# One ring of PSUM banks, weight splits in pieces, decay differences on ScalarE, and wide products in every second pair of the gate stage

## The chip, the cores and the metric

The kernel runs on one core of one Trainium2 chip. The metric is device time in microseconds (us), the median of several executions. Engines are named as in the profile: PE (TensorE, matmuls), PEld (its weight loads), DVE (VectorE), ACT (ScalarE), POOL (GpSimd), SP (SyncE, which issues all transfers here).

## The reference, cut to what matters

One layer of a hybrid decoder block on 256 positions of width 1024, in float32:

```python
h    = rms_norm(x, norm1_g)
proj = h @ w_in                          # q | k | v | z | xBC | dt | gate_attn | gate_ssd
A    = causal attention(rms_norm(q), rms_norm(k), v)        # 16 heads, ALiBi, one block of 256 keys
# state-space mixer, 8 groups of 4 heads, one chunk of 256 positions:
xs, bm, cm = split(silu(causal_conv(xBC)))
a    = softplus(dt + dt_bias) * -exp(a_log);  acum = cumsum(a)
lmat = exp(where(causal, acum[t] - acum[s], -inf))          # the decay between two positions
y    = einsum(cm @ bm.T, lmat, xs * dt) + d_skip * xs;  y = y * silu(z)
S    = y * rsqrt(mean(y * y, group) + eps) * ssd_norm_g
x    = x + (sigmoid(g_attn) * (A @ w_attn_o) + sigmoid(g_ssd) * (S @ w_ssd_o)) @ w_out
# expert layer: 8 heads pick 16 of 16384 single-neuron experts
xn   = rms_norm(x, norm2_g);  q = xn @ w_peer_q
eidx, gw = top16 over sums of top16(q1 @ keys1), top16(q2 @ keys2), softmax
x    = x + sum over picks of gw * gelu(xn . u_tab[eidx]) * v_tab[eidx]
```

## The kernel before

**Matmuls and weight splits.** Every large product is done in float32r with both operands split into a high and a low part, in three terms (high x high, high x low, low x high). The weights stream in as 392 tiles of 128 x 1024 (512 KB each), in the order of use. `ahead` (L115) keeps the loads five and the splits three tiles ahead of PE: ACT copies a tile to its high part `wh` (L128), and DVE (L135) or, for one tile in four and later in three, POOL (L130) subtracts it to get the low part `wl`. The activations' two parts lie beside each other (`hT`, `xx`: 8 blocks of 2 x 256 columns).

**Two forms of a product.** In the narrow form (`product_T` L162, `u_pair` L1040) each of a tile's eight weight blocks makes three matmuls of 256 columns, 24 in all. In the wide form (`wide`, L176) each high block makes one matmul of 512 columns over both parts of the activations, and each low block one of 256, 16 in all. The wide form leaves its result in two halves of a bank, which ACT (a copy) and DVE (an add) then bring together.

**Stages.** From 14 to 295 us: for each of eight groups the projections q/k, v, x, B/C and z, each followed by generators (`attention`, `conv`, `zgate`, `ssd`) that `tick` advances one step per half tile of products, so that the small operations of attention and mixer lie between the large products on PE. After the eight groups come the gate projections, the output projections, the norm and the query projection. From 438 us: the products with `u_tab`, 64 pairs of tiles. While the top-16 picks are made, pairs 0 to 26 take the wide form (`u_wide`, L1029); after that comes the gate stage (pairs 27 to 63, 638 to 883 us), in which each pair is narrow (`u_pair`) and is followed by up to one `gate_group` (L1077): matmuls of one-hot matrices (`oh`, `og`, made by DVE, L1067 and L1072) into a bank `psg`, by which DVE multiplies the gelu already stored (L1088) or which ACT stores (L1090). The last 348 us are the products with `v_tab` (L1136 to L1138).

**PSUM.** `ps_tile` (L229) hands out the eight banks from three rings: 3 "mm" for the large products, 2 "tr" for transposes, 3 "at" for the other small matmuls. A tile waits until the readers of the one that had its bank before are done. In the "tr" ring, the first transposed attention weights `pp` of a group, the second `pp`, and the transposed mixer output `pty` follow one another.

**The mixer's decay.** In `ssd` (L644), `ar` is the cumulative sum along the row, broadcast by a DMA from memory, and `nac` the negated sum of each position. `seg` (L668) makes min(ar + nac, 0) on DVE, `damp` (L674) the exponential on ACT and the product with the masked scores on DVE. Later DVE scales `y` by the group norm `ry` (L734), which POOL computes as a power (L223).

**Order of the work.** Engines work off their queues in order. The framework's scheduler sets the order on DVE, ACT and POOL; PE follows the program text.

Of the kernel before, what the change touches and what calls it, by code (L numbers as in the profile page):

```python
# [9 lines left out]
F32 = mybir.dt.float32  # L10
# [50 lines left out]
def tile_hybrid_block(ctx: ExitStack, tc: tile.TileContext, x, n1g, wblk, wdt, qkg, cw, cb, dtb,  # L61
# [167 lines left out]
    def ps_tile(tag, name):  # L229
        return psum.tile([128, 512], F32, name=name, tag=tag, bufs={"mm": 3, "tr": 2, "at": 3}[tag])  # L230

    with tc.tile_pool(name="pa", bufs=1) as pa, ExitStack() as ctx2:
# [76 lines left out]
        def turned_x(xn, tt):  # L309
            pt = ps_tile(("tr", "at")[tt], "ptx").rearrange("p (c t) -> p c t", c=4)  # L310
# [105 lines left out]
        nac = pa.tile([128, 2, 32], F32, name="nac")  # L416
# [11 lines left out]
        def decay():  # L428
# [34 lines left out]
            ps = ps_tile("tr", "psdtn")  # L463
# [31 lines left out]
            pc = ps_tile("at", "pscum")  # L495
# [3 lines left out]
            pr = ps_tile("at", "pscumT")  # L499
# [4 lines left out]
            A.activation(nac, pc[:, :64].rearrange("p (a h) -> p a h", a=2), AF.Copy, scale=-1.0)  # L504
# [5 lines left out]
        def attention(g):  # L510
# [19 lines left out]
            pt = half(ps_tile("tr", "ptq"))  # L530
# [42 lines left out]
            def turn(hh):  # L573
                pp[hh] = ps_tile("tr", "pp")
# [30 lines left out]
            po = ps_tile("at", "po")  # L605
# [38 lines left out]
        def ssd(g):  # L644
# [10 lines left out]
            pt = half(ps_tile("tr", "ptx"))  # L655
# [31 lines left out]
            pc = ps_tile("at", "pcb")  # L687
# [14 lines left out]
            py = half(ps_tile("at", "py"))  # L702
# [12 lines left out]
            pt = half(ps_tile("tr", "ptn"))  # L715
# [21 lines left out]
            pt = half(ps_tile("tr", "pty"))  # L737
# [93 lines left out]
        def norm2(tt, po):  # L831
# [3 lines left out]
            yield from norm_T(pm, tt, ss2[:, tt:tt + 1], n2, xh, xl, ("tr", "at")[tt])  # L835
# [54 lines left out]
    def head_scores(h, ps):  # L890
        qT = tk.tile([128, 2, T], F32, name="pqT", tag="pqT")
        if h == 0:
# [3 lines left out]
            ps = ps_tile("tr", "pqt").rearrange("p (c t) -> p c t", c=2)  # L896
# [13 lines left out]
        p2 = ps_tile("tr", "pss").rearrange("p (a n) -> p a n", a=4)  # L910
# [90 lines left out]
    def turned_picks(tt, srcs):  # L1001
# [4 lines left out]
        pt = ps_tile("tr", "ptk").rearrange("p (a t) -> p a t", a=4)  # L1006
# [96 lines left out]
    for jp in range(64):  # L1103
        (u_wide if start is None else u_pair)(jp)
# [17 lines left out]
    py = [ps_tile(("at", "at", "at", "mm")[i], f"py{i}") for i in range(4)]  # L1122
# [94 lines left out]
```

## Time and profile before

| | |
|---|---|
| Median of 3 executions | 1237.66 us (1237.06 to 1240.53) |
| Profiled execution | 1237.04 us, of which the span from first to last instruction is 1235.3 us |
| PE busy | 1217.6 us (99%) |
| DVE busy | 930.1 us (75%) |
| ACT busy | 668.9 us (54%) |
| POOL busy | 233.6 us (19%) |
| PE's share of the chain that ended last | 84% (DVE 9%, ACT 3%) |

A matmul's end is modelled and matmuls overlap, so the busy time of PE says little by itself. What a matmul costs is read from the time between the starts of neighbours, and what PE loses from its idle time before an instruction.

### The profile page before, as it was taken

What the parts mean: (1) busy time and instruction counts of PE and PEld (TensorE: products, weight loads), DVE (VectorE), ACT (ScalarE), POOL (GpSimd) and SP (SyncE); (2) the same over time, 40 slices, a digit from 0 to 9 for tenths busy, and PEclk for the clock granted to TensorE, in tenths of its full rate; (3) what the DMA queues carried; (4) which work ended last, traced back from release to release, by engine and by line L of the source; (5) the groups of instructions that cost most, each with busy time, mean ns of one, the idle gap of its engine ahead of it and who ended that gap; (6) DMA issues with size and microseconds to landing.
All of it is one profiled execution on the core that took longest, in us unless ns stands there. A gap on an engine that the chain in (4) does not pass through costs nothing.

```text
span 1235.3 us, 21224 instructions
## 1 busy us (share of the span) xinstructions
PE 1217.6 (99%) x8152; PEld 1093.6 (89%) x8152; DVE 930.1 (75%) x1721; ACT 668.9 (54%) x1108; POOL 233.6 (19%) x112
## 2 busy tenths in 40 slices
PE   9999999999999999999999999999999999999998
PEld 7989989898888988888889999999988888888887
DVE  6888989799566677899898898999755555555554
ACT  5666666677644455656655454444445445445442
POOL 3212223221232222233232222222000000000000
PEclk9999999999999999999999999999999999999999
DMA  5444444444555464546544444444555555555553
GB/s 197 162 170 148 154 170 155 155 147 137 177 205 188 136 222 159 197 161 202 195 163 171 171 159 166 155 155 154 180 195 187 201 191 188 200 192 189 200 189 120
DMA packets 60342, 215.07 MB, mean 174 GB/s; under 512 B 7600, under 2 KB 8144, under 8 KB 60112
## 3 DMA queue, kind: packets, MB, share of 16 engines
q1 hardware_dynamic: 60240, 213.71, 50.4%
q8 instruction: 64, 1.05, 0.3%
q14 instruction: 38, 0.31, 0.1%
HBM read 212.60 MB, written 1.08 MB: 173 GB/s over the span
## 4 chain that ended last, share of the span: by engine, by line
PE 84%; DVE 9%; ACT 3%; issue 2%; DMA 1%; POOL 0%; DVEq 0%; POOLq 0%
PE py L1136 9%; PE py L1138 9%; PE py L1137 9%; PE psu L189 7%; PE psu L1047 6%; PE psu L1048 6%; PE psu L1049 6%; PE psu L191 3%; PE psqk L207 2%; PE psg L1085 2%; PE pS L189 2%; PE psg L189 2%; PE psq L189 2%; DVE acc L626 2%; DVE wl L135 2%
## 5 line engine op out<-in xcount | busy, mean ns | idle before, releaser
L128 ACT ACTIVATE wh<-wr 128x1024 fp32r<-128x1024 f32 x390 | 411.0, 1055 | 221.1 <-PE py L1138 83.2
L135 DVE TENSOR_TENSOR wl<-wr,wh 128x1024 fp32r<-128x1024 f32 x312 | 383.0, 1229 | 134.8 <-ACT wh L128 133.8
L130 POOL TENSOR_TENSOR wl<-wr,wh 128x1024 fp32r<-128x1024 f32 x78 | 201.5, 2583 | 525.7 <-ACT wh L128 446.3
L1136 PE MATMUL py<-wh,hh 128*128 128x512 f32 x512 | 199.2, 389 | 0.0
L1137 PE MATMUL py<-wl,hh 128*128 128x512 f32 x512 | 199.2, 389 | 0.0
L1138 PE MATMUL py<-wh,hl 128*128 128x512 f32 x512 | 199.2, 389 | 0.0
L1047 PE MATMUL psu<-xx,wh 128*128 128x256 f32 x592 | 170.0, 287 | 0.0
L1048 PE MATMUL psu<-xx,wh 128*128 128x256 f32 x592 | 167.4, 283 | 0.0
L1049 PE MATMUL psu<-xx,wl 128*128 128x256 f32 x592 | 167.3, 283 | 0.0
L1138 PEld LDWEIGHTS py<-wh,hl 128*128 128x128 f32 x512 | 96.1, 188 | 20.1
L1136 PEld LDWEIGHTS py<-wh,hh 128*128 128x128 f32 x512 | 96.1, 188 | 19.8
L1137 PEld LDWEIGHTS py<-wl,hh 128*128 128x128 f32 x512 | 96.1, 188 | 19.8
L1048 PEld LDWEIGHTS psu<-xx,wh 128*128 128x128 f32 x592 | 113.5, 192 | 0.0
L1049 PEld LDWEIGHTS psu<-xx,wl 128*128 128x128 f32 x592 | 113.4, 192 | 0.0
L1047 PEld LDWEIGHTS psu<-xx,wh 128*128 128x128 f32 x592 | 113.3, 191 | 0.0
L189 PE MATMUL psu<-xx,wh 128*128 128x512 f32 x432 | 109.3, 393 | 0.5 <-DVE gA L1037 0.5
L189 PEld LDWEIGHTS psu<-xx,wh 128*128 128x128 f32 x432 | 77.3, 189 | 14.6 <-DVE gA L1037 1.1
L1128 ACT ACTIVATE hh<-gA 128x512 fp32r<-128x512 f32 x64 | 40.4, 632 | 88.8 <-PE py L1137 88.7
L1129 DVE SCALAR_TENSOR_TENSOR hl<-gA,hh 128x512 fp32r<-128x512 f32 x64 | 44.4, 694 | 52.3 <-ACT hh L1128 52.3
L191 PEld LDWEIGHTS psu<-xx,wl 128*128 128x128 f32 x432 | 59.0, 190 | 4.3
L191 PE MATMUL psu<-xx,wl 128*128 128x256 f32 x432 | 60.4, 282 | 0.0
L1072 DVE TENSOR_TENSOR og<-oh,g 128x1024 f16<-128x1024 f16 x64 | 58.0, 946 | 1.0
(324 smaller groups left out, 2211.7 us busy)
## 6 DMA issues: line engine op xcount, KB each, us to landing
wr<-in_u_tab SPq DMA_DIRECT2D x128, 512.0 KB, 3.3
wr<-in_v_tab SPq DMA_DIRECT2D x128, 512.0 KB, 3.2
wr<-in_wblk SPq DMA_DIRECT2D x88, 512.0 KB, 3.3
wr<-in_wso SPq DMA_DIRECT2D x16, 512.0 KB, 4.0
wr<-in_wpq SPq DMA_DIRECT2D x16, 512.0 KB, 3.8
ar<-acT SPq DMA_DIRECT2D x8, 512.0 KB, 4.9
wr<-in_wao SPq DMA_DIRECT2D x8, 512.0 KB, 3.4
wr<-in_wou SPq DMA_DIRECT2D x8, 512.0 KB, 3.5
```

Of the source, the lines that this page charges most:

```text
L128: K(A.activation(h, r, AF.Copy))
L130: state["pool"] = nc.gpsimd.tensor_tensor(lo, r, f32(h), op=OP.subtract)
L135: state["wl"] = K(V.tensor_tensor(lo, r, f32(h), op=OP.subtract))
L189: mm(ps, h[:, c], x[:, k], start=k == 0, stop=k == 8 * n - 1)
L191: mm(ps[:, 1], lo[:, c], x[:, k, 0], start=False, stop=False)
L1047: mm(ps[:, jj], h[:, c], xh[:, c], start=c == 0, stop=False)
L1048: mm(ps[:, jj], h[:, c], xl[:, c], start=False, stop=False)
L1049: mm(ps[:, jj], lo[:, c], xh[:, c], start=False, stop=c == 7)
L1072: V.tensor_tensor(og[:, i], oh[:, 1], g2[:, i, t].rearrange("p (g e) -> p g e", e=2)[:, :, None, :] .to_broadcast([128, 4, 128, 2]), op=OP ...
L1136: mm(o, hh[:, jj, s], h[:, c], start=j == 0, stop=False)
L1137: mm(o, hh[:, jj, s], lo[:, c], start=False, stop=False)
L1138: mm(o, hl[:, jj, s], h[:, c], start=False, stop=j == 127)
```

## The change

The two rings "tr" (2 banks) and "at" (3) become one ring "ax" of 5; all tiles of both take the tag "ax", as do the four `py` accumulators of the last stage (one of them was "mm"). POOL's splits are made in four pieces of 256 columns, each an instruction, and PE waits for the piece that it reads. The decay difference moves from DVE to ACT: relu(acum[s] - ar), and the exponential takes the scale -1. The scaling of `y` moves from DVE to ACT. In the gate stage every second pair (27, 29, ... 63) takes the wide form; where gate values are already stored, its gelu goes to a scratch tile and is multiplied in.

```diff
             if i == 121 or (2 < i < n_u + 128 and not 116 <= i < 124 and i % (3 if i >= 88 else 4) == PS[i >= 88]):
-                state["pool"] = nc.gpsimd.tensor_tensor(lo, r, f32(h), op=OP.subtract)
-                if behind:
-                    after(state["pool"], behind[1])
+                for c in range(4):
+                    q = slice(256 * c, 256 * c + 256)
+                    state["pool"] = nc.gpsimd.tensor_tensor(lo[:, q], r[:, q], f32(h)[:, q], op=OP.subtract)
+                    if behind and c == 0:
+                        after(state["pool"], behind[1])
...
-        return psum.tile([128, 512], F32, name=name, tag=tag, bufs={"mm": 3, "tr": 2, "at": 3}[tag])
+        return psum.tile([128, 512], F32, name=name, tag=tag, bufs={"mm": 3, "ax": 5}[tag])
...
-            A.activation(nac, pc[:, :64].rearrange("p (a h) -> p a h", a=2), AF.Copy, scale=-1.0)
+            A.activation(pac, pc[:, :64].rearrange("p (a h) -> p a h", a=2), AF.Copy)
...
             def turn(hh):
-                pp[hh] = ps_tile("tr", "pp")
+                pp[hh] = ps_tile("ax", "pp")
...
-                V.tensor_scalar(e[:, 0:256], ar[:, r], nac[:, 0, h:h + 1], 0.0, op0=OP.add, op1=OP.min)
-                V.tensor_scalar(e[:, 256:384], ar[:, r, 128:256], nac[:, 1, h:h + 1], 0.0, op0=OP.add, op1=OP.min)
+                A.activation(e[:, 0:256], ar[:, r], AF.Relu, bias=pac[:, 0, h:h + 1], scale=-1.0)
+                A.activation(e[:, 256:384], ar[:, r, 128:256], AF.Relu, bias=pac[:, 1, h:h + 1], scale=-1.0)
...
-                A.activation(e, e, AF.Exp)
+                A.activation(e, e, AF.Exp, scale=-1.0)
...
-                V.tensor_scalar(y[:, tt], y[:, tt], rr[:, tt:tt + 1], None, op0=OP.mult)
+                A.activation(y[:, tt], y[:, tt], AF.Copy, scale=rr[:, tt:tt + 1])
...
         (_, _, dst), = halves(2 * jp, 2 * jp + 2)
+        td = done["t"]
+        to = pb.tile([128, 2, T], F32, name="gel", tag="gel", bufs=2) if td else dst
         for jj in range(2):
             ps = half(ps_tile("mm", "psu"))
             wide(ps, 1, xx)
-            A.activation(dst[:, jj], ps[:, 1], AF.Copy)
-            V.tensor_tensor(dst[:, jj], dst[:, jj], ps[:, 0], op=OP.add)
-        A.activation(dst, dst, AF.Gelu)
+            A.activation(to[:, jj], ps[:, 1], AF.Copy)
+            V.tensor_tensor(to[:, jj], to[:, jj], ps[:, 0], op=OP.add)
+        if td < T:
+            A.activation(dst[:, :, td:], to[:, :, td:], AF.Gelu)
+        if td:
+            A.activation(to[:, :, :td], to[:, :, :td], AF.Gelu)
+            V.tensor_tensor(dst[:, :, :td], dst[:, :, :td], to[:, :, :td], op=OP.mult)
...
-        (u_wide if start is None else u_pair)(jp)
+        (u_wide if start is None or jp % 2 else u_pair)(jp)
...
-    py = [ps_tile(("at", "at", "at", "mm")[i], f"py{i}") for i in range(4)]
+    py = [ps_tile("ax", f"py{i}") for i in range(4)]
```

**Order on ACT, group 0's mixer.** The place is where the broadcast sums `ar` of group 0 have landed and its decay is made; `e` is the decay, `acc` and `u` the convolution, `qkT` the turned q and k of group 1, `wh` a weight's high part. Before:

```order
L620 ACTIVATE u<-psxs_796 128x512
L622 ACTIVATE acc<-psxs_796,cbs,cws 128x256 x2
L676 ACTIVATE e<-e 128x384 x2
L128 ACTIVATE wh_987<-wr_881 128x1024
L538 ACTIVATE qkT<-ptq,qkgs 128x256 x2
L630 ACTIVATE th<-acc 128x512
L128 ACTIVATE wh_993<-wr_935 128x1024
```

The same place on ACT now:

```order
L623 ACTIVATE u<-psxs_805 128x512
L625 ACTIVATE acc<-psxs_805,cbs,cws 128x256
L675 ACTIVATE e<-ar,pac 128x256
L676 ACTIVATE e<-ar,pac 128x128
L675 ACTIVATE e<-ar,pac 128x256
L676 ACTIVATE e<-ar,pac 128x128
L625 ACTIVATE acc<-psxs_805,cbs,cws 128x256
L541 ACTIVATE qkT<-ptq,qkgs 128x256 x2
L128 ACTIVATE wh_999<-wr_890 128x1024
L633 ACTIVATE th<-acc 128x512
L680 ACTIVATE e<-e 128x384 x2
```

Four differences (L675, L676) are new on ACT, and the two exponentials (L680, before L676) now stand behind half a convolution, `qkT`, a weight and `th`.

**Order on DVE, at group 0's mixer output.** `yT` is what PE's transposes `ptn` wait for, `bc` the convolved B and C of group 1. Before:

```order
L135 TENSOR_TENSOR wl_1126<-wr_985,wh_1125 128x1024
L626 SCALAR_TENSOR_TENSOR acc<-u,cws,acc 128x253
L671 TENSOR_SCALAR e<-ar,nac 128x256
L712 SCALAR_TENSOR_TENSOR yT<-xs,dks,py 128x256 x2
L633 SCALAR_TENSOR_TENSOR bc<-th,acc 128x512
```

The same place on DVE now:

```order
L138 TENSOR_TENSOR wl_1138<-wr_997,wh_1137 128x1024
L572 RECIPROCAL rs<-sums 128x2
L636 SCALAR_TENSOR_TENSOR bc<-th,acc 128x512
L716 SCALAR_TENSOR_TENSOR yT<-xs,dks,py 128x256 x2
L728 TENSOR_TENSOR y<-ptn,zz 128x512
```

The difference `e` in front of `yT` is gone, and `bc` has come in front of it.

**Order on DVE, gate stage.** The place is between the multiplications by 144 and by 152 columns of gate values; `gel` is the scratch tile, `oh` and `og` the one-hot matrices. Now:

```order
L1098 TENSOR_TENSOR gA_7841<-gA_7841,psg 128x34x4
L1077 TENSOR_TENSOR oh<-iot,selT 128x2048
L1043 TENSOR_TENSOR gel<-gel,psu 128x256
L1082 TENSOR_TENSOR og<-oh,g_5558 128x1024 x2
L138 TENSOR_TENSOR wl_9831<-wr_9743,wh_9830 128x1024
L1043 TENSOR_TENSOR gel<-gel,psu 128x256
L1098 TENSOR_TENSOR gA_5555<-gA_5555,psg 128x64x4 x2
```

Before, the same rows stood there without the two additions L1043. On PE nothing changes its place: the sequence of tiles that its matmuls write is the same, with 16 matmuls in place of 24 for each tile of 19 pairs. On SP one `ar` transfer goes one place earlier.

## Rows read from the trace of the kernel before

**Rows 1.** Stretches: busy time of each engine (instructions), granted clock, DMA share, GB/s.

```profile
...
14.00:295.00 281.00, 271.65 (x2214) 254.28 (x2213) 239.82 (x489) 189.69 (x389) 69.78 (x38) 0.99 0.45 155
...
638.00:883.00 245.00, 245.00 (x2293) 243.49 (x2292) 219.80 (x305) 117.34 (x221) 63.58 (x25) 1.00 0.48 163
```

**Rows 2.** What PE waited for: us in total, times, longest us.

```profile
...
PE ptn L718 <- DVE yT L712: 3.0, 1, 3.0
PE pp L576 <- DVE yy L749: 3.0, 3, 1.9
...
PE pp L576 <- ACT pT L580: 1.2, 1, 1.2
...
PE pp L576 <- ACT wh L128: 0.9, 1, 0.9
PE pp L576 <- ACT acc L622: 0.7, 1, 0.7
```

**Rows 3.** Timeline 153 to 158 us: start, us, engine, line, operation, tiles [idle <-releaser].

```profile
...
156.09 0.87 DVE L749 SCALAR_TENSOR_TENSOR yy<-pty,sg,yy 128x256 fp32r<-128x256 f32 x2
...
157.10 0.52 PE L576 MATMUL pp<-ident,p 128*128 128x128 f32 x3 [1.93 <-DVE yy L749]
```

**Rows 4.** Timeline 80 to 85.5 us.

```profile
...
81.19 2.44 POOL L130 TENSOR_TENSOR wl<-wr,wh 128x1024 fp32r<-128x1024 f32 x1 [15.39 <-ACT wh L128]
81.35 2.43 DVE L671 TENSOR_SCALAR e<-ar,nac 128x256 f32<-128x256 f32 x1
...
83.70 0.86 DVE L712 SCALAR_TENSOR_TENSOR yT<-xs,dks,py 128x256 f32<-128x256 f32 x2
```

**Rows 5.** Timeline 641 to 643.2 us, PE: a narrow product.

```profile
...
641.16 0.28 PE L1047 MATMUL psu<-xx,wh 128*128 128x256 f32 x1
...
642.96 0.28 PE L1047 MATMUL psu<-xx,wh 128*128 128x256 f32 x1
```

**Rows 6.** Timeline 500 to 512 us, PE: wide products.

```profile
...
502.20 2.00 PE L189 MATMUL psu<-xx,wh 128*128 128x512 f32 x8
...
507.79 2.00 PE L189 MATMUL psu<-xx,wh 128*128 128x512 f32 x8
```

**Rows 7.** Groups by form: busy us, mean ns of one | idle before, releasers.

```profile
...
L128 ACT ACTIVATE wh<-wr 128x1024 fp32r<-128x1024 f32 x390 | 411.0, 1055 | 221.1 <-PE py L1138 83.2 <-PE psu L1048 37.0 <-issue 32.0
...
L130 POOL TENSOR_TENSOR wl<-wr,wh 128x1024 fp32r<-128x1024 f32 x78 | 201.5, 2583 | 525.7 <-ACT wh L128 446.3 <-ACT gA L1055 13.4 <-DVE og L1072 8.2
...
L1047 PE MATMUL psu<-xx,wh 128*128 128x256 f32 x592 | 170.0, 287 | 0.0
...
L189 PE MATMUL psu<-xx,wh 128*128 128x512 f32 x432 | 109.3, 393 | 0.5 <-DVE gA L1037 0.5
...
L191 PE MATMUL psu<-xx,wl 128*128 128x256 f32 x432 | 60.4, 282 | 0.0
...
L1037 DVE TENSOR_TENSOR gA<-gA,psu 128x256 f32<-128x256 f32 x54 | 22.1, 409 | 6.1 <-ACT gA L1036 6.1
...
L1036 ACT ACTIVATE gA<-psu 128x256 f32<-128x256 f32 x54 | 20.5, 379 | 31.2 <-PE psu L189 31.2
...
L671 DVE TENSOR_SCALAR e<-ar,nac 128x256 f32<-128x256 f32 x32 | 17.6, 550 | 3.5 <-DMA ar<-acT 3.5
...
L571 ACT ACTIVATE p<-p,rs 128x256 f32<-128x256 f32 x16 | 7.9, 495 | 0.0
...
L571 ACT ACTIVATE p<-p,rs 128x128 f32<-128x128 f32 x16 | 6.3, 391 | 0.8 <-DVE rs L569 0.8
...
L362 POOL TENSOR_TENSOR wl<-wr,wh 128x512 fp32r<-128x512 f32 x2 | 2.5, 1290 | 2.5 <-ACT wh L336 2.5
```

**Rows 8.** What ACT waited for, 14 to 295 us.

```profile
...
ACT e L676 <- DVE e L672: 13.1, 9, 2.8
```

**Rows 9.** Timeline 781 to 785 us: the gate stage.

```profile
...
780.91 3.50 DVE L1072 TENSOR_TENSOR og<-oh,g 128x1024 f16<-128x1024 f16 x2
...
781.32 2.54 POOL L130 TENSOR_TENSOR wl<-wr,wh 128x1024 fp32r<-128x1024 f32 x1 [8.19 <-ACT wh L128]
```

More of the change, by code (lines that the diff above doesn't have):

```diff
@@ L309, in turned_x @@
         def turned_x(xn, tt):
-            pt = ps_tile(("tr", "at")[tt], "ptx").rearrange("p (c t) -> p c t", c=4)
+            pt = ps_tile("ax", "ptx").rearrange("p (c t) -> p c t", c=4)
             for c in range(4):
@@ L415, in tile_hybrid_block @@
         dth = pa.tile([128, 2, 32], F32, name="dth")
-        nac = pa.tile([128, 2, 32], F32, name="nac")
+        pac = pa.tile([128, 2, 32], F32, name="pac")
         dram = ctx.enter_context(tc.tile_pool(name="dr", bufs=1, space=bass.MemoryType.DRAM))
@@ L462, in decay @@
             yield
-            ps = ps_tile("tr", "psdtn")
+            ps = ps_tile("ax", "psdtn")
             for tt in range(2):
@@ L494, in decay @@
                 yield
-            pc = ps_tile("at", "pscum")
+            pc = ps_tile("ax", "pscum")
             mm(pc[:, 0:32], mask[:, 0:128], av[:, 0], start=True, stop=True)
@@ L498, in decay @@
             mm(pc[:, 32:64], mask[:, 0:128], av[:, 1], start=False, stop=True)
-            pr = ps_tile("at", "pscumT")
+            pr = ps_tile("ax", "pscumT")
             mm(pr[:32, 0:128], av[:, 0], mask[:, 0:128], start=True, stop=True)
@@ L529, in attention @@
             yield
-            pt = half(ps_tile("tr", "ptq"))
+            pt = half(ps_tile("ax", "ptq"))
             for tt in range(2):
@@ L548, in score @@
                         if a == 0:
-                            sc[hh] = ps_tile("at", "sc")
+                            sc[hh] = ps_tile("ax", "sc")
                         mm(sc[hh][:, a:b], q[:, a:a + 128], k[:, :b - a], start=True, stop=True)
@@ L604, in attention @@
             v = vsb[g // 2]
-            po = ps_tile("at", "po")
+            po = ps_tile("ax", "po")
             for i, (qs, ks_) in enumerate((((0, 256), (0, 256)), ((128, 256), (256, 384)))):
@@ L654, in ssd @@
             yield
-            pt = half(ps_tile("tr", "ptx"))
+            pt = half(ps_tile("ax", "ptx"))
             for tt in range(2):
@@ L686, in ssd @@
             yield
-            pc = ps_tile("at", "pcb")
+            pc = ps_tile("ax", "pcb")
             mm(pc[:, 0:256], bc[:, 0, 0:128], bc[:, 1], start=True, stop=True)
@@ L701, in ssd @@
             yield
-            py = half(ps_tile("at", "py"))
+            py = half(ps_tile("ax", "py"))
             for ct in range(2):
@@ L714, in ssd @@
             yield
-            pt = half(ps_tile("tr", "ptn"))
+            pt = half(ps_tile("ax", "ptn"))
             for tt in range(2):
@@ L733, in ssd @@
             for tt in range(2):
-                V.tensor_scalar(y[:, tt], y[:, tt], rr[:, tt:tt + 1], None, op0=OP.mult)
+                A.activation(y[:, tt], y[:, tt], AF.Copy, scale=rr[:, tt:tt + 1])
             yield
             yield
-            pt = half(ps_tile("tr", "pty"))
+            pt = half(ps_tile("ax", "pty"))
             for c in range(2):
@@ L834, in norm2 @@
             V.tensor_reduce(ss2[:, tt:tt + 1], ss4[:, tt], axis=AX.X, op=OP.add)
-            yield from norm_T(pm, tt, ss2[:, tt:tt + 1], n2, xh, xl, ("tr", "at")[tt])
+            yield from norm_T(pm, tt, ss2[:, tt:tt + 1], n2, xh, xl, "ax")
         n2 = tg[:, 0, 0:4].rearrange("p a t -> p (a t)")
@@ L895, in head_scores @@
             yield
-            ps = ps_tile("tr", "pqt").rearrange("p (c t) -> p c t", c=2)
+            ps = ps_tile("ax", "pqt").rearrange("p (c t) -> p c t", c=2)
             for f in range(2):
@@ L909, in head_scores @@
         yield
-        p2 = ps_tile("tr", "pss").rearrange("p (a n) -> p a n", a=4)
+        p2 = ps_tile("ax", "pss").rearrange("p (a n) -> p a n", a=4)
         for tt in range(2):
@@ L1005, in turned_picks @@
         t = slice(128 * tt, 128 * tt + 128)
-        pt = ps_tile("tr", "ptk").rearrange("p (a t) -> p a t", a=4)
+        pt = ps_tile("ax", "ptk").rearrange("p (a t) -> p a t", a=4)
         for i, src in enumerate(srcs):
@@ L1080, in gate_group @@
             t0 = 8 * q + 4 * f
-            pg = ps_tile("at", "psg").rearrange("p (t j) -> p t j", t=4)
+            pg = ps_tile("ax", "psg").rearrange("p (t j) -> p t j", t=4)
             for t in range(4):
```

## The prediction

> **What bounds the kernel now.** I read the busy times by stretch first. In both stretches that the change works in, PE is the fullest engine: 271.65 of 281 us from 14 to 295 us, and 245.00 of 245 in the gate stage (638 to 883 us), where its weight loads are busy for 243.49 and DVE for 219.80 [rows 1]. So a gain has only two sources: PE stands still less, or its instructions get shorter. Busy time does not price the second, since matmuls overlap. The view of what PE waited for prices the first, and it is short: one wait of 3.0 us of the transposes `ptn` for DVE's `yT`, and six waits of `pp` of 3.0, 1.2, 0.9 and 0.7 us, together 5.8 [rows 2]. The rest of that view is small. After the start-up it names no weight split, so the splits run far enough ahead; DVE, ACT and POOL count only where one of these waits ends.
>
> A wait costs a little more than its idle time. That time is counted from the modelled end of the matmul before, 0.28 us after its start, where the next would have started after 0.12 us [rows 5]. So each wait costs 0.16 more: 6.8 us for the six, 3.2 for `ptn`.
>
> **The change part by part.**
>
> *One ring of banks: 6.8 us less.* The releasers named for `pp` differ (DVE `yy`, ACT `pT`, a copy of weights, `acc`), but the timeline shows the same place each time: the second `pp` of a group. In group 3 it starts at 157.10, right behind the two `yy` (156.09 to 156.96), which read `pty` [rows 3]. `pty` had the bank two places before in the ring "tr"; in the other five waits too `yy` ends within 0.2 us of the start of `pp`, the last at about 293 us. The attention weights themselves are there earlier. In the ring of five, the tile five places before the second `pp` is `ptq` or a score tile, whose readers come before the softmax that makes `pp`'s input, so they are done. All six waits should go. Below: nothing is gained if another tile in the ring holds on as long. Above: no more than 6.8. I take 6.8. Next in line behind `pp` is the score tile's successor, and those readers had no wait in this trace.
>
> *Decay differences and `y` to ACT, as DVE sees it: 1.7 us less.* The wait of `ptn` has one cause: in front of `yT`, DVE's difference `e` takes 2.43 us (81.35 to 83.78), the whole time that POOL's split runs (81.19 to 83.63) [rows 4]; the mean of these differences is 550 ns [rows 7]. DVE stands still while POOL works on SBUF. The difference leaves DVE, but by the order `bc` now comes in front of `yT`. It is a pass over 512 columns with both inputs in SBUF; two passes of `yT` over 256 took 0.86 [rows 4], so I take 0.7. Saved: 2.43 - 0.7 = 1.7 us of the 3.2. Ends: 0.3, if `bc` also waits for two pieces of POOL, and 3.2.
>
> *The same, as ACT sees it: 2.5 us more.* The nearest rows for the new operations are ACT's scalings with a scale per partition, 495 ns for 256 columns and 391 for 128 [rows 7]. Each group gets eight differences, 4 x (495 + 391) = 3.54 us, and two scalings of `y`, 0.99: 4.5 us a group, 36 in all. ACT has 281 - 189.69 = 91 us of idle time in this stretch, and 13.1 us of that was spent waiting for the very differences [rows 1, 8]. In seven groups I cost it at nothing: `ar` has landed before, and the block of differences can use ACT's gaps. In group 0 it is in series: `ar` has just landed, and the first two exponentials now stand behind four differences (1.77), a weight's copy (1.06 [rows 7]) and four halves of convolution and q/k of about 0.5 each by the 495 ns row: 4.8 us. Before they stood behind DVE's differences of two heads, about 1.2 as estimated from 344 to 550 ns a piece. So `py`, which needs them, is up to 3.6 us late. Ends: 0, if PE comes that much later anyway, and 5.4 with the second block added (1.77). I take 2.5, near the middle. The scaling of `y` also makes ACT wait for POOL's power, behind up to four pieces of a split; queued behind it are a weight's copy and the next group's convolution. The copies are ahead of PE, so that costs nothing while the wait is below a tile or two.
>
> The Trainium skill ("ScalarE: Activation LUTs", Rules for kernel authors) speaks against this edit: relu, max, min and add belong on VectorE, not ScalarE. The rows do not show it: 495 ns on ACT against a mean of 550 on DVE, in which waits for POOL such as the 2.43 us are contained. If it holds here, the edit adds more work than it removes, and the sum is that of the first rival.
>
> *Pieces on POOL: 0.* A split of 1024 columns takes 2583 ns, one of 512 takes 1290 [rows 7], so by these rows a piece of 256 takes about 0.65 and four take as long as one did; a fixed cost of 0.1 each would add 0.4. A DVE instruction that meets POOL then waits at most for a piece. In the gate stage two `og` took 3.50 us beside a split of 2.54 [rows 9], where the mean of one is below 1 us. That is relief for DVE, which PE does not wait for there. Ends: -1 (the norm before the query projection, where POOL and DVE meet too) and +1.
>
> *Wide products in 19 pairs: 3.3 us less.* The tempting price is the mean of one: 24 x 287 ns = 6.9 us a tile narrow, 8 x 393 + 8 x 282 = 5.4 wide [rows 7], so 1.5 us x 38 tiles = 57 us. But these are times in flight. By starts, 15 narrow matmuls go from 641.16 to 642.96, 0.120 each, so 24 take 2.88 us [rows 5]; wide tiles begin 5.59 us apart for two, 2.795 each [rows 6]. The difference is 0.085 x 38 = 3.3 us. Both forms stream the same columns, 24 x 256 = 8 x 512 + 8 x 256; only the cost of each of eight matmuls goes. Each wide tile adds a copy of 379 ns on ACT and an add of 409 on DVE [rows 7], 14.4 and 15.5 us in all. ACT has half its time free there. DVE goes from 219.80 to 235 of about 242, less what the pieces give back. I cost this at nothing; without cover it is the second rival. Ends: 0 to 3.5.
>
> *Nothing* for the `py` tiles and the other tags, for which PE has no wait to lose, and for PE's order, which is the same.
>
> Sum: -6.8 - 1.7 + 2.5 - 3.3 = -9.3 us. The profiled execution took 1237.04 us (span 1235.3), so 1227.7. The median of the runs is 0.6 above it, 1237.66, and gives 1228.4. I predict 1228.
>
> **Rivals.**
>
> *ACT takes DVE's place (slower).* Mechanism: ACT works in order, its differences come in blocks of four in front of `pT` and the exponentials, and `y` waits for POOL; PE then stands at `pp`, `po` or `py` in each of the eight groups. For it: 189.69 + 36 = 226 of some 272 us (281 less the gains), 83%, and each block is 1.77 us. Against it: ACT's 13.1 us of waiting for differences go, and `pp` hardly waited for ACT's results before. If half of the 4.5 us a group reaches PE, 8 x 2.25 = 18 us, against gains of 6.8 + 1.7 + 3.3 = 11.8: 1237.7 + 6.2 = 1244. It decides from 1.5 us a group.
>
> *DVE fills up in the gate stage (no change).* If POOL's pieces follow one another so closely that DVE waits for all four, the 3.50 us of `og` [rows 9] stay and the 15.5 us of adds come on top in a stage that is 90% busy on DVE. With half of them in the later, fuller part, and that half reaching PE, 7.8 us: 1228.4 + 7.8 = 1236.
>
> *The ring only moves the wait (it doesn't do what it says).* Five banks serve eleven tiles a group as before; a score or `py` tile held long could stop a transpose that it could not stop before. Against it: no tile of "at" made PE wait in this trace. It gives back 6.8: 1228.4 + 6.8 = 1235.
>
> *More than forecast.* No give-back on ACT, the whole 3.2 of `ptn`, 1 us at the second norm: 1228.4 - 2.5 - 1.5 - 1 = 1223.
>
> *PE is bound by its weight loads in the gate stage.* They are busy for 99% of it [rows 1], and the wide form has 16 in place of 24. Then a third of the 2.88 us would go, 0.96 x 38 = 36.5 us in place of the 3.3: 1195. Against it stands the wide stage itself: 2.795 us with 16 loads [rows 6]. The Trainium skill ("Perfetto Trace Analysis", Identifying the Most-Contended Engine) says that matmul busy time misleads and that the busy share of weight loads is one of the good measures. The first half agrees with these rows (57 us against 3.3); the second would give 1195 here, and the 2.795 speaks against it.
>
> **How the numbers follow.** Forecast 0.66 (its own range 1224 to 1232), more than forecast 0.08, the ring 0.08, DVE 0.09, ACT 0.08, weight loads 0.01. What a measurement of this kernel can tell from no change is about 0.3%, 3.7 us. Below 1234 lie the forecast, "more" and the loads, and a little of the ring and DVE cases: 0.77. Within 3.7 us of 1237.7 lie most of these two, 0.15. Above lies ACT: 0.08. The range leaves out the ACT case and a little below: 1222 to 1237.
>
> **What would show it.** Right: no row of `pp` over 0.3 us among PE's waits, and `ptn` below 2; the stretch from 14 to the first output projection about 6 us shorter, the gate stage about 3; tiles in wide pairs 2.80 apart; `og` near 0.7 to 1.3 us beside POOL; ACT's differences near 495 and 391 ns. Wrong: waits of PE for `m`, `p` or `pT` in several groups (ACT); waits of `psg` for `og`, or of `psu` for `gel` (DVE); waits of `ptx`, `pcb` or `sc` for a bank (the ring).

## The result, and the profile after

| | before | changed kernel | changed, whole splits (found below) |
|---|---|---|---|
| Median, us | 1237.53 (1235.16 to 1240.64, 20 executions) | 1228.02 (1226.70 to 1236.40, 20) | 1224.26 (1223.98 to 1225.10, 4) |
| Ratio to before, 95% interval | | 0.9928 [0.9919, 0.9938] | 0.9890 [0.9876, 0.9904] |
| Span of the profiled execution, us | 1235.3 | 1225.8 | 1222.5 |

The change is 8.9 us faster (7.7 to 10.0), where 9.3 was forecast. The starts of PE's matmuls divide the span into stretches:

| us from ... to ... | before | changed | whole splits |
|---|---|---|---|
| start to the first `psv` | 18.5 | 18.9 | 19.3 |
| first `psv` to the first gate-matrix product (the eight groups) | 268.9 | 260.4 | 259.0 |
| from there to the first output projection `pA` | 51.1 | 50.6 | 50.0 |
| `pA` to the query projection | 92.4 | 92.6 | 92.6 |
| query projection to the first `psg<-og` | 219.3 | 219.4 | 219.3 |
| first to last `psg<-og` (the gate stage) | 226.9 | 224.7 | 224.3 |
| last `psg<-og` to the first `py<-wh,hh` | 5.9 | 6.7 | 5.7 |
| from there to the end | 352.4 | 352.7 | 352.3 |

The gain lies where it was forecast: 9.1 us from the first `psv` to `pA` (8.7 if the start, 0.4 later, is counted), and 2.2 in the gate stage, of which 0.8 is given back behind it. What PE waited for in the changed kernel, against [rows 2] (us in total, times, longest):

```profile
PE ptn L722 <- DVE yT L716: 1.5, 1, 1.5
...
PE py L1146 <- ACT gA L1100: 0.8, 1, 0.8
...
PE pp L579 <- ACT p L574: 0.4, 1, 0.4
```

The six waits of `pp` are gone; the 0.4 left is at the start of group 0, and before had it too. `ptn` waits half as long as in [rows 2], and `py` is new. The two stretches of [rows 1], with the same columns:

```profile
14.00:288.00 274.00, 271.88 (x2230) 255.36 (x2230) 212.24 (x416) 212.74 (x463) 78.12 (x92) 1.00 0.48 159
631.00:873.00 242.00, 241.21 (x1982) 224.01 (x1981) 222.03 (x337) 125.34 (x254) 108.74 (x99) 1.00 0.48 163
```

In the groups PE stands only 2.1 us in place of 9.4, and ACT's busy time has passed DVE's. In the gate stage DVE is busy for 92% of the time, and POOL for 109 us in place of 64. The changed lines, by form (busy us, mean ns | idle before), against [rows 7]:

```profile
L133 POOL TENSOR_TENSOR wl<-wr,wh 128x256 fp32r<-128x256 f32 x312 | 283.9, 940 | 436.4 <-ACT wh L128 430.3 <-ACT gA L1065 4.9 <-issue 1.1
...
L675 ACT ACTIVATE e<-ar,pac 128x256 f32<-128x256 f32 x32 | 16.2, 506 | 2.2 <-DMA ar<-acT 2.2
...
L676 ACT ACTIVATE e<-ar,pac 128x128 f32<-128x128 f32 x32 | 12.6, 395 | 0.0
...
L738 ACT ACTIVATE y<-y,ry 128x256 f32<-128x256 f32 x16 | 7.4, 506 | 4.1 <-POOL ry L226 4.1
```

ACT's new operations cost what was read from its scalings (495 and 391 ns). A piece on POOL does not: 0.94 us, not 0.65, so a split takes 3.8 us in place of 2.6. The wide form is as priced; the first matmuls of two tiles of a late pair (start and duration in us; a row merges the eight or two matmuls that its end names):

```profile
841.77 2.00 PE L192 MATMUL psu<-xx,wh 128*128 128x512 f32 x8
...
844.56 0.63 PE L192 MATMUL psu<-xx,wh 128*128 128x512 f32 x2
```

They begin 2.79 us apart, as in [rows 6]; 34 of the 38 added tiles lie between the first and the last `psg<-og`.

Where the 0.8 us behind the gate stage come from, timeline of the changed kernel at its end:

```profile
871.03 0.67 DVE L1069 TENSOR_TENSOR gA<-gA,gel 128x496 f32<-128x496 f32 x1
871.62 1.06 DVE L1098 TENSOR_TENSOR gA<-gA,psg 128x248 f32<-128x248 f32 x3
872.12 0.18 ACT L1100 ACTIVATE gA<-psg 128x8 f32<-128x8 f32 x1 [2.23 <-DVE gA L1098]
872.39 0.63 ACT L1138 ACTIVATE hh<-gA 128x512 fp32r<-128x512 f32 x1
...
873.07 0.50 PE L1146 MATMUL py<-wh,hh 128*128 128x512 f32 x1 [0.79 <-ACT gA L1100]
```

DVE is behind, a small copy on ACT waits 2.23 us for it, `hh` stands behind that copy, and PE's first down product waits for `hh`. This is the mechanism of the rival on a full DVE, at a tenth of its price.

One thing in the trace of before the prediction did not read: the granted clock behind the wait of `ptn`. Columns as in [rows 1]; before, then the changed kernel:

```profile
84.00:86.00 2.00, 1.78 (x8) 1.57 (x9) 2.00 (x7) 0.53 (x1) 0.00 (x0) 0.50 0.64 219
86.00:88.00 2.00, 2.00 (x14) 2.00 (x14) 1.02 (x2) 0.90 (x2) 0.00 (x0) 0.68 0.14 51
```

```profile
84.00:86.00 2.00, 2.00 (x20) 2.00 (x19) 1.27 (x2) 2.00 (x7) 1.73 (x3) 1.00 0.39 147
86.00:88.00 2.00, 2.00 (x18) 1.95 (x17) 1.23 (x4) 2.00 (x7) 0.70 (x1) 1.00 0.57 193
```

Before, PE ran at the lower of its two levels after it had stood for 3 us: 2 x 0.50 + 2 x 0.32, with 2 x 0.04 in the window ahead, makes 1.7 us lost, of which 0.2 falls into the wait itself. The changed kernel stands 1.5 us there, and the clock stays at 1.0.

### The profile page after: what moved, and what is told of

Same layout as the page of the kernel before. It is cut to its first block, busy times and chain, and to the rows that moved or that the text cites. A ratio compares the mean times of both kernels' runs of the same rounds, so it can differ in the third digit from the quotient of the medians.

```text
span 1225.8 us, 21037 instructions
## 1 busy us (share of the span) xinstructions
PE 1214.8 (99%) x7848; PEld 1075.1 (88%) x7848; DVE 902.2 (74%) x1679; ACT 705.4 (58%) x1226; POOL 311.8 (25%) x346
## 4 chain that ended last, share of the span: by engine, by line
PE 85%; DVE 7%; DMA 2%; issue 2%; POOL 2%; ACT 1%; DVEq 0%; ACTq 0%; POOLq 0%
PE psu L192 11%; PE py L1148 9%; PE py L1147 9%; PE py L1146 9%; PE psu L194 5%; PE psqk L210 3%; PE psz L210 3%; PE pS L192 2%; PE psg L192 2%; PE psq L192 2%; PE psu L1057 2%; PE psu L1058 2%; PE psu L1059 2%; DVE wl L138 2%; PE pO L210 2%
## 5 line engine op out<-in xcount | busy, mean ns | idle before, releaser
L138 DVE TENSOR_TENSOR wl<-wr,wh 128x1024 fp32r<-128x1024 f32 x312 | 393.9, 1264 | 132.6 <-ACT wh L128 132.0
L133 POOL TENSOR_TENSOR wl<-wr,wh 128x256 fp32r<-128x256 f32 x312 | 283.9, 940 | 436.4 <-ACT wh L128 430.3
L192 PE MATMUL psu<-xx,wh 128*128 128x512 f32 x736 | 190.0, 395 | 0.5 <-DVE gA L1043 0.5
L192 PEld LDWEIGHTS psu<-xx,wh 128*128 128x128 f32 x736 | 130.7, 189 | 22.7 <-DVE gA L1043 0.9
L194 PEld LDWEIGHTS psu<-xx,wl 128*128 128x128 f32 x736 | 100.4, 190 | 7.6
L194 PE MATMUL psu<-xx,wl 128*128 128x256 f32 x736 | 102.8, 282 | 0.0
L1057 PE MATMUL psu<-xx,wh 128*128 128x256 f32 x288 | 82.8, 288 | 0.1
L1058 PE MATMUL psu<-xx,wh 128*128 128x256 f32 x288 | 81.5, 283 | 0.0
L1059 PE MATMUL psu<-xx,wl 128*128 128x256 f32 x288 | 81.4, 283 | 0.0
L1057 PEld LDWEIGHTS psu<-xx,wh 128*128 128x128 f32 x288 | 55.1, 191 | 0.3 <-ACT gA L1065 0.3
L1058 PEld LDWEIGHTS psu<-xx,wh 128*128 128x128 f32 x288 | 55.2, 192 | 0.1
L1059 PEld LDWEIGHTS psu<-xx,wl 128*128 128x128 f32 x288 | 55.2, 192 | 0.0
```

What stands on the lines that cost most here:

```text
L133: state["pool"] = nc.gpsimd.tensor_tensor(lo[:, q], r[:, q], f32(h)[:, q], op=OP.subtract)
L192: mm(ps, h[:, c], x[:, k], start=k == 0, stop=k == 8 * n - 1)
L194: mm(ps[:, 1], lo[:, c], x[:, k, 0], start=False, stop=False)
L1057: mm(ps[:, jj], h[:, c], xh[:, c], start=c == 0, stop=False)
L1058: mm(ps[:, jj], h[:, c], xl[:, c], start=False, stop=False)
L1059: mm(ps[:, jj], lo[:, c], xh[:, c], start=False, stop=c == 7)
```

## The experiments

My theory after the result: ring, shorter `ptn` and shorter tiles give what was forecast, ACT costs nothing, the clock gives 1.7 us more, and the pieces and a full DVE take some of it back. The first four runs do one part of the change alone, the next three undo one part each, the last five take up the full DVE, the pieces and the clock. Differences in us are the ratio's, of 1237.5, where the text does not say that they are the medians'.

**The ring alone.**

```diff
-        ... bufs={"mm": 3, "tr": 2, "at": 3}[tag])
+        ... bufs={"mm": 3, "ax": 5}[tag])
...
```

All tiles of both rings, and the four `py` of the last stage, take the tag "ax".

> The kernel before with one ring of five banks and nothing else. Theory (the six waits of the second `pp` are waits for the bank that `yy` holds): 6.8 us less, about 1230.7, ratio 0.9945; no row of `pp` above 0.5 us among PE's waits, while the wait of `ptn` for `yT` stays near 3 us, and the gate stage stays as long as before. Rival (the wait is only handed to another tile of the common ring): ratio 0.999 to 1.001, the same microseconds under `ptx`, `pcb`, `sc` or `py`. Rival (DVE's late `yy` is late because DVE is loaded, and what it works for comes late too): some of the six go, some stay under another name, 2 to 4 us less.

Measured: 1231.30, ratio 0.9955 [0.9942, 0.9969], 5.6 us less. No row of `pp` is left among PE's waits, the rest reads:

```profile
PE ptn L718 <- DVE yT L712: 3.0, 1, 3.0
...
PE ptq L533 <- DVE qn L527: 0.9, 1, 0.9
```

The stretches up to `pA` are 6.3 us shorter and all later ones are the same within 0.4. The theory holds. The 0.9 of `ptq` is the little that DVE's lateness still costs; both rivals fall.

**ACT's share alone.**

```diff
-                V.tensor_scalar(e[:, 0:256], ar[:, r], nac[:, 0, h:h + 1], 0.0, op0=OP.add, op1=OP.min)
...
+                A.activation(e[:, 0:256], ar[:, r], AF.Relu, bias=pac[:, 0, h:h + 1], scale=-1.0)
...
-                V.tensor_scalar(y[:, tt], y[:, tt], rr[:, tt:tt + 1], None, op0=OP.mult)
+                A.activation(y[:, tt], y[:, tt], AF.Copy, scale=rr[:, tt:tt + 1])
```

> The kernel before with the decay differences and the scaling of `y` on ScalarE and nothing else. Theory (DVE's difference beside POOL's split delays `yT`; ACT has the room): `ptn` falls from 3.0 to about 1.5 us or below; with DVE lighter the two `yy` come a little earlier, so the six waits of `pp` lose 0 to 3 us: in all 1.5 to 4.5 us less, 1233 to 1236, ratio 0.9964 to 0.9988. Rival (my term of 2.5 us for ACT, or more: `py`, `pp` or `po` wait for `m`, `p` or `pT`): 1236 to 1240, ratio 0.999 to 1.002, with such waits named.

Measured: 1233.65, ratio 0.9974 [0.9964, 0.9985], 3.2 us less. Its waits and the clock behind `ptn`:

```profile
PE pp L576 <- DVE yy L750: 3.7, 3, 1.8
PE pp L576 <- ACT acc L622: 1.4, 1, 1.4
...
PE pp L576 <- ACT e L673: 1.0, 1, 1.0
PE ptn L719 <- DVE yT L713: 0.8, 1, 0.8
```

```profile
84.00:86.00 2.00, 2.00 (x18) 1.95 (x17) 1.24 (x4) 2.00 (x7) 0.70 (x1) 1.00 0.64 215
```

`ptn` loses 2.2 of its 3.0 us and the clock stays up: 2.2 + 1.7 = 3.9, against 3.8 found in the groups. The waits of `pp` are as long as before (6.1 us), five places in place of six. So no wait of `py` shows ACT's lateness (what is left at `ptn` is taken up below), and the gain was mine to see in [rows 4]: DVE's difference behind POOL's split, and what the clock did after it.

**Wide tiles alone.**

```diff
-        (u_wide if start is None else u_pair)(jp)
+        (u_wide if start is None or jp % 2 else u_pair)(jp)
```

> The kernel before with wide products in every second pair beside the gate matrices, and nothing else; POOL's splits are whole. Theory (a wide tile is 0.076 to 0.085 us shorter, DVE has the room): 2.9 to 3.2 us less before what the first down product gives back; 1235, ratio 0.9976. Rival (DVE fills up: beside a whole split a DVE instruction waits longer than beside a piece): the adds of 15.5 us make `og` or `gel` late, PE waits at `psg` or `psu` and the gain is gone or more: ratio 1.000 to 1.004, with rows of `psg` or `psu` above 1 us.

Measured: 1235.12, ratio 0.9987 [0.9978, 0.9996], 1.6 us less (0.5 to 2.7). The median is the theory's, the ratio a little short of it. In its profile the gate stage is 2.6 us shorter and the way to `py` 0.2 shorter, and no wait of `psg` appears: beside whole splits, every second pair fits DVE. The profiled execution is one of the longest (1237.93): its groups, which the edit does not touch, take 272.1 us in place of 268.9, with a granted clock of 0.5 for 6.8 us behind `ptn` and 3.4 us behind a `pp`.

**Pieces alone.**

```diff
-                state["pool"] = nc.gpsimd.tensor_tensor(lo, r, f32(h), op=OP.subtract)
+                for c in range(4):
+                    q = slice(256 * c, 256 * c + 256)
+                    state["pool"] = nc.gpsimd.tensor_tensor(lo[:, q], r[:, q], f32(h)[:, q], op=OP.subtract)
...
```

> The kernel before with POOL's splits in four pieces and nothing else. Theory (PE hardly waits for what the pieces can free): -1 to +1 us, ratio 0.999 to 1.001; the pieces take 0.94 us each as in the changed kernel, so a split takes 3.8 us in place of 2.6; the difference `e` beside a split takes about 1 us in place of 2.43, and `ptn` loses 1 to 2 of its 3.0 us. Rival (DVE takes up as much from four longer-running pieces as from one split): `ptn` stays near 3 us and the waits of `pp` grow: 1 to 4 us more.

Measured: 1234.48, ratio 0.9982 [0.9973, 0.9991], 2.2 us less, outside the theory's bounds and of the other sign than the rival's.

```profile
PE ptn L721 <- DVE yT L715: 1.6, 1, 1.6
PE pp L579 <- DVE yy L752: 1.4, 1, 1.4
```

`e` beside a split takes 0.81 us in place of 2.43, so `ptn` loses 1.4 us, as expected; what was not, `pp` waits 2.1 us less too, since `yy` comes earlier. The groups are 2.5 us shorter. By themselves the pieces do help DVE where PE waits for it.

**Without the ring**: the changed kernel with the two rings of before.

> The changed kernel with the two rings of before (two and three banks) put back. Theory (the ring's gain does not hang on the other parts, since `yy` stays just as late): 1233 to 1235, that is 5 to 7 us over the changed kernel, with five or six waits of `pp` named again. Rival (pieces and ACT's share have made DVE early enough by themselves: alone, the pieces left 3.8 us of such waits and ACT's share 6.1): 1230 to 1232, two to four waits.

Measured: 1235.24 (1232.23 to 1240.87), ratio 0.9987 [0.9971, 1.0003], 7.2 us over the changed kernel by medians. Three long waits of `pp` are named again (2.0, 1.5 and 1.0 us, the first followed by a granted clock of 0.5), which is the rival's number, but the groups are 5.6 us longer and the whole is 0.2 us over the theory's range. The three waits are 4.5 us and the lower clock 1.7, together a little more than the 5.6. So both are half right: beside the other parts the ring still saves most of the waits that it saves alone (5.8), and the clock behind one of them makes up the rest. Some 1.4 us more lie in the gate stage, where `psg` waits 1.5 for ACT.

**Without pieces**: the changed kernel with whole splits.

```diff
-                for c in range(4):
-                    q = slice(256 * c, 256 * c + 256)
-                    state["pool"] = nc.gpsimd.tensor_tensor(lo[:, q], r[:, q], f32(h)[:, q], op=OP.subtract)
...
+                state["pool"] = nc.gpsimd.tensor_tensor(lo, r, f32(h), op=OP.subtract)
...
```

> The changed kernel with POOL's splits whole. Theory (a piece takes 0.94 us, so DVE meets POOL for 3.8 us a split in place of 2.6; with the difference off DVE nothing long stands in front of `yT`): `ptn` waits 0.8 us as with ACT's share alone, not 1.5, so the groups are 0.5 to 1 us shorter; in the gate stage nothing changes by more than 0.5; 1227 to 1228. Rival (DVE's room in the gate stage comes from the pieces): `og`, or `hh` behind it, comes later and PE waits 1 to 4 us more there: 1229 to 1232.

Measured: 1224.26, ratio 0.9890 [0.9876, 0.9904], 3.8 us below the changed kernel by medians (4.7 by the ratios), and its executions lie within 1.1 us where those of the changed kernel lie within 9.7. The order of instructions on PE, DVE and ACT is the same in both. Beyond both expectations. Its waits of PE:

```profile
PE ptn L719 <- DVE yT L713: 0.5, 1, 0.5
PE psu L189 <- DVE gA L1040: 0.4, 2, 0.2
```

By the first matmuls of each stretch the pieces cost 1.3 us in the groups, 0.5 behind them, 0.4 in the gate stage, 1.0 at `py` and 0.4 after it; the start goes 0.4 the other way. DVE is busier here in the gate stage (225.9 of 240 us) and yet nothing comes late.

Of the 1.3 us in the groups 1.0 is the shorter wait of `ptn`, and the timelines show where that comes from. First use of `ar` in group 0 and `yT`, here and then in the changed kernel:

```profile
66.06 0.51 ACT L672 ACTIVATE e<-ar,pac 128x256 f32<-128x256 f32 x1 [1.10 <-DMA ar<-acT]
81.85 0.87 DVE L713 SCALAR_TENSOR_TENSOR yT<-xs,dks,py 128x256 f32<-128x256 f32 x2
```

```profile
67.00 0.51 ACT L675 ACTIVATE e<-ar,pac 128x256 f32<-128x256 f32 x1 [2.19 <-DMA ar<-acT]
68.98 0.49 DVE L629 SCALAR_TENSOR_TENSOR acc<-u,cws,acc 128x255 f32<-128x255 f32 x1 [1.57 <-ACT acc L625]
82.80 0.86 DVE L716 SCALAR_TENSOR_TENSOR yT<-xs,dks,py 128x256 f32<-128x256 f32 x2
```

ACT stands until `ar` has landed, then makes four differences and only then the half convolution `acc` for which DVE waits; from there to `yT` DVE's longest gap is 0.15 us. In eight traces with the differences on ACT, with whole splits or cut ones, `yT` starts 15.8 us after this first use. (The run with a late `ptn` below puts work between them and is left out.) So the wait of `ptn` follows the landing of `ar`, 0.94 us later in the changed kernel's trace, and the pieces change nothing between the two. That the pieces delay this transfer is possible: it lands 9.6 to 11.0 us after the copy `ac` that it starts from in the six traces with cut splits in the groups, and 9.3 to 9.7 in the eight with whole ones. How they would do so is not shown.

**Without ACT's share**: the changed kernel with differences and `y` on DVE.

> The changed kernel with decay differences and the scaling of `y` back on DVE. Theory (what ACT's share still gives beside ring and pieces is `ptn` and the clock behind it: with the pieces alone PE stood 1.6 us there and the granted clock then fell to 0.5 for some 3.5 us, with the full change it stood 1.5 and the clock stayed at 1.0): 1 to 3 us more, 1229 to 1231. Rival (my term of 2.5 us of ACT's lateness is there and only hidden by other gains): 1 to 3 us less, 1225 to 1227.

Measured: 1234.11 (1229.76 to 1237.32), ratio 0.9964 [0.9948, 0.9980], 6.1 us over the changed kernel by medians (4.5 by the ratios): the sign of the theory, more than its size. In the profile only 1.3 us of it lie in the groups (`ptn` waits 1.6, the clock stays at 1.0); the rest is waits of `psu` for DVE (3.1 us) and of `py` for `hh` (2.1), and 1.7 us of lower clock at the query projection, all in stages that the edit does not touch. The same waits of `psu` and `py` stand in the run with late pieces below, so they are laid to the pieces here, and this run does not price ACT's share. The difference between whole splits (259.0 us in the groups) and the ring alone (263.5) does: 4.5 us.

**All pairs wide, with pieces and with whole splits.** The edit is `u_wide(jp)` for every pair, once in the changed kernel and once with whole splits.

> The changed kernel with the other pairs of the gate stage wide too, about 34 tiles more. Theory (DVE has no more room: 222.0 of 242 us busy, and 34 adds of 0.41 us make 236; `og` is already only 2 to 5 us ahead of its product at the end): the tiles are 34 x 0.076 = 2.6 us shorter, but PE waits for `og`, or at the first down product, 3 to 10 us more: 1228 to 1236. Rival (DVE still keeps ahead): 1225.5, with no wait of PE over 1.5 us there.

> The changed kernel with whole splits and every pair of the gate stage wide. With whole splits and every second pair wide DVE was busy for 226 of 240 us there and PE had no wait over 0.4 us. Theory (DVE is the limit, pieces or not: 34 more adds of 0.41 make 240 of 237): PE waits 3 us or more for `og` or `gel` and the 2.6 us of shorter tiles are lost: 1224 to 1229. Rival (the waits of the kernel with all pairs wide came from the pieces): 1221.5 to 1223, no wait over 1 us.

Measured: with pieces 1230.86, ratio 0.9946 [0.9928, 0.9965]; with whole splits 1230.40, ratio 0.9938 [0.9926, 0.9951]. By medians that is 2.8 and 6.1 us over every second pair, the second beyond the theory's 1229. The second one's waits, and its gate stage:

```profile
PE psg L1092 <- DVE og L1079: 5.3, 4, 2.6
```

```profile
640.00:880.00 240.00, 234.01 (x1646) 202.02 (x1644) 231.96 (x368) 133.55 (x285) 67.92 (x23) 0.99 0.50 160
```

DVE is the limit with either kind of split: `og` is late four times near the end of the stage (with pieces once, 2.9 us), and behind the longest wait the granted clock falls to 0.5 from 868 to 870 us. The rival falls. The prediction's rival of a full DVE is real, and the change stops just short of it.

**Two halves in place of four pieces.**

```diff
-                for c in range(4):
-                    q = slice(256 * c, 256 * c + 256)
+                for c in range(2):
+                    q = slice(512 * c, 512 * c + 512)
```

> The changed kernel with each of POOL's splits in two pieces of 512 columns in place of four of 256. By the rows of before a split of 512 takes 1290 ns, so two take no longer than one of 1024. Theory (the pieces cost because four take 3.8 us in place of 2.6, so that DVE meets POOL more often): halves are as good as whole splits, 1224 to 1225.5, with a spread of a microsecond or two. Rival (what costs is that a split in pieces meets several DVE instructions in turn, however long it takes): between whole and four, 1226 to 1227.5, and executions some microseconds apart.

Measured: 1225.41 (1224.94 to 1225.91), ratio 0.9896 [0.9882, 0.9910]. A half takes 1493 ns, a split 3.0 us. That lies between 2.6 and 3.8 as the time lies between whole and four pieces, nearer to whole: the theory's range, though 1.2 us over whole. The rival's scatter of some microseconds is not there.

**Pieces only from the hidden units' tables on.**

```diff
-                for c in range(4):
-                    q = slice(256 * c, 256 * c + 256)
+                n_p = 4 if i >= n_u else 1
+                for c in range(n_p):
+                    q = slice(1024 // n_p * c, 1024 // n_p * (c + 1))
```

> The changed kernel with the splits whole up to the query projection and in four pieces from the first hidden unit's table on. Theory (the cost of the pieces lies in the stages where DVE is 90% busy, and there above all in the executions in which `gA`, `og` or `hh` comes late): 1226 to 1227.5, executions some microseconds apart, with waits of `psu`, `psg` or `py` for `gA` or `hh`. Rival (it lies in the groups, where the one profile shows 1.3 us and behind them 0.5): 1223.5 to 1225, as with whole splits throughout.

Measured: 1227.98, ratio 0.9913 [0.9898, 0.9927], executions from 1225.88 to 1234.38. The profiled one is the longest of them and shows how it happens:

```profile
PE psu L193 <- DVE gA L1044: 3.6, 5, 1.5
PE py L1147 <- ACT hh L1139: 1.5, 1, 1.5
...
PE psu L195 <- POOL wl L134: 1.3, 3, 0.7
```

In its timeline a piece that starts alone takes 0.75 us; the third of this split starts 0.2 us after DVE's own split of 1024 columns and takes 1.72:

```profile
589.04 0.75 POOL L134 TENSOR_TENSOR wl<-wr,wh 128x256 fp32r<-128x256 f32 x1 [6.01 <-ACT wh L128]
...
590.44 1.72 POOL L134 TENSOR_TENSOR wl<-wr,wh 128x256 fp32r<-128x256 f32 x1
```

```profile
590.23 1.34 DVE L139 TENSOR_TENSOR wl<-wr,wh 128x1024 fp32r<-128x1024 f32 x1 [0.59 <-ACT wh L128]
```

So between two pieces DVE gets in front, and POOL waits. The split ends 3.8 us after it began, and PE waits for it twice (0.7 and 0.2 us; the third wait, 0.4, is for an earlier one). The waits for `gA` follow at 619 to 630 us; that they come from such splits is argued, not shown. The waits are the theory's, but the median lies 0.5 over its range, as high as with pieces throughout (1228.02). So by medians all of the price lies in the late stages, and what the profiles show in the groups (260.4 us with pieces there, 259.4 here, 259.0 with whole splits) is not seen in them. Executions 8.5 us apart do not settle it.

**A late `ptn`**, to test the clock: whole splits, and in the first group

```diff
+            if g == 0:
+                for _ in range(4):
+                    V.tensor_tensor(yT, py, xs, op=OP.add)
```

> The changed kernel with whole splits, and in the first group four adds of 512 columns on DVE in front of `yT`, about 0.6 us each, whose result `yT` overwrites: `ptn` should wait about 3 us again as in the kernel before. Theory (such a wait costs itself and then the clock behind it, which in the kernel before stood at 0.5 from 84 to 87 us): 2.4 us of waiting and 1.5 to 2 of clock, together 3.9 to 4.4 more than the 1224.3 with whole splits: 1228.2 to 1228.7, granted clock near 0.6 between 84 and 88 us. Rival (the clock fell for another reason, ACT's or DVE's load in that stretch): 2.4 more, 1226.7, granted clock 1.0.

Measured: 1224.28, ratio 0.9886 [0.9870, 0.9903]. This tests neither: the transposes also moved on PE behind another product, to 85.9 us, and waited 0.7 us only.

```profile
PE ptn L722 <- DVE yT L716: 0.7, 1, 0.7
```

What is left for the clock are the fourteen traces. In them, up to PE's last matmul, a granted clock of 0.5 appears only at the end of a wait of PE or up to 2.3 us behind one: at `ptn` after 3.0 us (before, the ring alone, wide tiles alone) and after 1.6 (pieces alone), at `pp` after 1.9 and 2.0 (wide tiles alone, no ring), at `psg` after 2.6 (all wide, whole), and at the second norm after 0.9 in three. But the same 1.6 at `ptn` (without ACT's share), 1.9 at `pp` (before, 155 us), 0.9 at the norm (before), and even 2.9 at `psg` (all wide, with pieces) and 2.1 at `py` (without ACT's share) left it at 1.0. That the wait brings it down was not forced by an experiment, and why it follows in one trace and not in another stays open. Its price shows in the times too: of 54 executions of the kernel before beside these runs, the five with a mean granted clock of 1.000 took 1235.3 to 1235.7, where the medians are 1237.2 to 1238.2.

## Why the prediction was right

The forecast of 1228 held, the forecast case with it, and the ring, its largest term, did what was said. That the number came out within a microsecond is luck: up to `pA` 6.0 us were forecast and 8.7 measured, from the gate stage to the first `py` 3.3 and 1.4. Two terms were mis-sized in opposite directions and one was missing.

- *Ring, 6.8:* right. Alone it gave 5.6 (3.8 to 7.2); the bank of `pty` was the cause of all six waits.
- *`ptn`, 1.7:* right in size for the changed kernel (3.05 less 1.50 is 1.55), but "one cause" is too much. In the kernel before, too, DVE starts when `ar` lands and has no gap over 0.1 us from there to `yT` at 83.70, 18.3 us later:

```profile
65.37 0.58 DVE L671 TENSOR_SCALAR e<-ar,nac 128x256 f32<-128x256 f32 x1 [3.53 <-DMA ar<-acT]
```

  The difference beside POOL's split is one piece of that work. The 2.5 without pieces is the same way of 15.8 us behind an earlier `ar`.
- *ACT's lateness, 2.5 back:* wrong at `py`, where it is 0. The step that failed is "I take 2.5, near the middle". The exponentials were late nearly as worked out (3.3 us, counted from `ar`), but neither DVE nor PE was there yet. The first group before, then after (start, us; `m` is what `py` needs):

```profile
66.18 0.98 ACT L676 ACTIVATE e<-e 128x384 f32<-128x384 f32 x2 [1.46 <-DVE e L672]
...
71.09 1.01 DVE L678 TENSOR_TENSOR m<-e,cbm 128x384 f32<-128x384 f32 x2
...
74.43 0.87 PE L707 MATMUL py<-m,xdt 128*64 128x256 f32 x8
```

```profile
71.13 0.93 ACT L680 ACTIVATE e<-e 128x384 f32<-128x384 f32 x2
...
72.86 0.55 DVE L682 TENSOR_TENSOR m<-e,cbm 128x384 f32<-128x384 f32 x1
74.46 0.55 DVE L682 TENSOR_TENSOR m<-e,cbm 128x384 f32<-128x384 f32 x1
...
75.09 0.87 PE L711 MATMUL py<-m,xdt 128*64 128x256 f32 x8
```

  The second `m` ends at 75.01 in place of 72.10, 2.9 us later, and `py` still starts behind the product ahead of it: the 2.3 us of slack that before had at this place, and the 0.66 us by which all of PE's work here lies later, are used up to 0.08. The slack stood in the trace and should have been subtracted. Of the 2.9 us, 1.6 is `ar` landing later; 1.3 is DVE's queue standing for the half convolution behind ACT's four differences. Without a gap in DVE's work these 1.3 us reach `yT`, and so they are most of the 1.5 that `ptn` still waits: an estimate from the timelines, which no run tests. The lateness was there, but at another wait.
- *The clock behind `ptn`:* missing, 1.7 us. [rows 1] showed a mean of 0.99 in the stretch, and 1% of 281 us is about as much as the wait itself.
- *Pieces, 0:* the term that failed most. Beside the other parts they cost 3.8 us, outside the bounds of -1 to +1. The step was "by these rows a piece of 256 takes about 0.65": alone it takes 0.74, and with DVE's instructions in between 0.94 on average and up to 1.73. The relief was real, 2.2 us alone, but it went to the same waits that ring and ACT remove; together, only the cost is left. The Trainium skill ("SBUF — State Buffer", Who interferes with whom) says that a VectorE instruction that takes the ports shared with GpSimd contends with it: whoever issues first has them for the whole instruction, and the other is blocked. The runs agree, in both directions: DVE's 2.43 us beside POOL's 2.44 in [rows 4], and POOL's 1.72 beside DVE's 1.34 in the run with late pieces. Not every DVE instruction meets POOL, as the prediction's "DVE stands still" has it: in the trace of before the add `gA<-gA,psu`, which reads PSUM, takes 0.41 us alone and beside POOL, `og` 0.69 alone, 1.41 on average beside it and up to 2.90.
- *Wide tiles, 3.3:* 0.085 x 38 is 3.2; measured are 0.076 a tile by starts and 34 tiles in the stage, 2.6; the small waits and `py` take back 1.2 of it in the changed kernel, and nothing with whole splits.

Of the rivals, DVE's is the nearest miss, though `og` took 0.68 to 1.23 us beside POOL, as forecast; weight loads fall, with 224 of 242 us in place of 243 of 245 and PE no faster than its starts say.

So 9.5 us of span came as about 6.3 (ring), 4.5 (ACT's share, clock included) and 2.6 (tiles), less 3.3 that the pieces cost in the profiled pair. That makes 10.1. With whole splits the start came 0.8 later than before (the 3.3 holds the 0.4 that it is earlier with pieces), which leaves 9.3. Why the start is later is not shown.

## What to carry to other kernels

Before a lateness is priced, subtract the slack of the waiting instruction in the same trace: it stands between the end of its last input and its start. Then follow the queue that is late to the next wait that hangs on it, and back to the transfer that it starts from. Two cures for one wait don't add; test each part beside the others, since a part that helps alone (the pieces, 2.2 us) can be the one to take out of the whole (3.8 us). Behind a long wait of PE look at the granted clock as well, because a stretch at the lower level can cost 1.5 to 1.7 us on top.

## What the runs showed of the hardware

- Cutting a POOL operation into pieces lets DVE in between, and POOL then waits for DVE: 0.75 us alone, 1.72 when it starts just after a 1024-column subtraction on DVE.
- A wait of PE can be followed by a stretch at the lower clock, worth 1.5 to 1.7 us behind a wait of 3.0; behind 1.6 us at the same place one kernel had it and another had not, and a wait of 2.9 at another place was not followed by it.
- With the pieces, executions of the changed kernel differed by up to 9.7 us (20 of them); with whole splits by 1.1 (4), and the two others built on whole splits by 0.7 (4) and 1.1 (6).
